# A transformer layer with product-key experts: the up side of a second token tile is gathered

## The chip, the cores and the metric

One core of a Trainium2 chip runs the whole layer in one launch. The metric is the device time of that launch in microseconds (us); three runs of the kernel before gave 1610.23, 1615.54 and 1618.56 us.

## The reference, cut to what matters

512 tokens of width 1024 pass an attention half (shift and scale by a condition, projections, differential and windowed attention, output projection, layer norm) and then an expert half. Only the expert half is touched:

```
q      = h @ w_pq                      # 8 heads, two half queries of 128 each
scores = q . sub_keys                  # 128 keys for each half
top 16 of each half -> 256 sums -> top 16 of them: idx (of 16384 experts), g = softmax
a   = gelu(u_tab[idx] . h)             # the up side: 8 x 16 = 128 experts a token
out = sum (g * a) * v_tab[idx]         # the down side
x   = LayerNorm(alpha * x + gate2 * out)
```

`u_tab` and `v_tab` have 16384 rows of 1024 floats (64 MiB each). Everything is float32.

## The kernel before, in words

The 512 tokens are four tiles of 128. **Tile 0** is done by gather: for each of its 128 choices an indirect DMA on GpSimd's queue (`fetch`, L720) brings one row of `u_tab` for each token into a buffer `gb` (512 KB, 4 buffers), and VectorE multiplies it with the token rows `h2n` and sums along the row (L728); after gelu the same is done with `v_tab`, each row added to `acc0` with its weight (L738).

**Tiles 1 to 3** are dense. The 16384 experts are 128 blocks of 128. `u_block(e)` (L749) loads a 512 KB block of `u_T` into `raw` (3 buffers, `load_raw`), splits it into a rounded part `hi` (ScalarE, L80) and a rest `lo` (VectorE, L81), both float32r with 3 buffers each, and makes the up products of 384 tokens as three float32r products for each of 8 slices (`mm3`, L90 to L92, tile `st`, two PSUM buffers). Gelu writes them to `a_r` (L756), a ring of NB + 1 = 33 buffers. `v_block(n)` (L796) loads a block of `v_tab`, splits it in the same way, multiplies `a` with the block's gate weights from `gl` (L811), splits the product into `wh` (L816) and `wl` (L817), and `v_mm` adds 18 products of 512 columns to six PSUM banks (`acc`).

The gate weights reach `gl` by a one-hot build, `make_g` (L656): for 8 tokens at a time ("a unit") VectorE makes two one-hot tables `oh0` and `oh1`, ScalarE scales the one by the gate g (8 instructions, L677), TensorE multiplies them (8 plain f32 products of 128 columns, L681), and the two PSUM banks are copied to `stage`, one by ScalarE and one by VectorE (L684). Two units make a 1 MB write to `g_d` in DRAM. A tile takes 16 units. `topk` (L596) finds the 16 choices of a tile on VectorE.

The order: first the loop over e = 0 to NB + NS - 1 = 55, which has one `u_block`, a share of `topk` (`budget`), of `make_g` (GRATE units a block) and of the gather (`c2`). The first 32 results stay in the ring; those of the NS = 24 blocks after them go to DRAM as `a_d` (`keep`, L759), through the one buffer of the ring that is left. Then the loop over n = 0 to 127: for n < 72 a `u_block` and a `v_block` ("mixed"), after that `v_block` alone; the blocks in `a_d` come last and are read back as `a_b`. A share of the gather goes along with each n. `pull(gen, us)` takes steps from a generator until the costs that it yields use up the share. All loads and stores but the gathers are issued by SyncE's queue (SP), in one order; each engine works in the order of the program.

Of the kernel before, what the change touches and what calls it, by code (L numbers as in the profile page):

```python
# [11 lines left out]
F32 = mybir.dt.float32  # L12
# [25 lines left out]
GB = 8  # L38
NS = 24
GRATE = 1.25  # L40
LAST = 6


@with_exitstack
def layer(ctx: ExitStack, tc: tile.TileContext, A, out, dbg=None):
# [17 lines left out]
    x1_d = [dram.tile([P, D], F32, name=f"x1_d{t}") for t in range(NT)]  # L63
    h2_d = dram.tile([P, D], F32, name="h2_d")
    g2_d = dram.tile([1, D], F32, name="g2_d")
    a_d = [dram.tile([P, TD], F32, name=f"a_d{e}") for e in range(NS)]
    g_d = dram.tile([NTG, P, NKEY, TG], F32, name="g_d")
# [63 lines left out]

# [1 line left out]
    at_stack = ExitStack()  # L133
# [313 lines left out]

# [1 line left out]
    lt = at_stack.enter_context(tc.tile_pool(name="lt", bufs=1, reuse_waits="tile"))  # L449
# [48 lines left out]
    def post_x(t, pre, x1):  # L498
        nc.vector.tensor_mul(x1, pre, ln1g)
        nc.vector.tensor_add(x1, x1, ln1b)  # L500
        dma(x1_d[t], x1)
        if "x1" in dbg:
            dma(dbg["x1"][t * P:(t + 1) * P, :], x1)
        if t == 0:
            sc2row = row_of(lt, scale2, "rowtmp")
            h2 = pre
            nc.vector.tensor_mul(h2, x1, sc2row)
            sh2row = row_of(lt, cols(3), "rowtmp")
            nc.vector.tensor_add(h2, h2, sh2row)
            dma(h2_d, h2)  # L510
            g2row = row_of(lt, cols(5), "rowtmp")
            dma(g2_d, g2row[0:1, :])
# [20 lines left out]

# [1 line left out]
    sel = ctx.enter_context(tc.tile_pool(name="sel", bufs=1, reuse_waits="tile"))  # L535
    vals = sel.tile([P, NT, 16, K16], F32, name="vals")
# [45 lines left out]
    q_stack.close()  # L582
    pro.close()

# [1 line left out]
    psB = ctx.enter_context(tc.tile_pool(name="psB", bufs=1, space=bass.MemoryType.PSUM, reuse_waits="tile"))  # L586
    ring_stack = ExitStack()
    ring = ring_stack.enter_context(tc.tile_pool(name="ring", bufs=1, side="right", reuse_waits="tile"))
    gath = ctx.enter_context(tc.tile_pool(name="gath", bufs=1, reuse_waits="tile"))
    acts = {}  # L590
# [5 lines left out]
    def topk(t, pool):  # L596
# [31 lines left out]
        yield 1.8  # L628
        i01 = sel.tile([P, 2, H, K16], F32, name="i01", tag="i01", bufs=2)
        for s in range(2):  # L630
# [11 lines left out]
            yield 1.4  # L642
        g = sel.tile([P, H, K16], F32, name="g", tag="g", bufs=2)
        nc.vector.tensor_sub(g, tv, tv[:, :, 0:1].to_broadcast([P, H, K16]))
# [11 lines left out]
    def make_g(t, pool):  # L656
# [9 lines left out]
        for tg in range(P // TG):  # L666
            stage = pool.tile([P, NKEY, TG], F32, name="stage", tag="stage", bufs=2)
            for q in range(TG // 8):
# [9 lines left out]
                for u in range(2):  # L678
                    ps = accbank()
                    for i in range(4):  # L680
                        nc.tensor.matmul(ps[:, i * P:(i + 1) * P], oh1[:, 4 * u + i, :], go[:, 4 * u + i, :],  # L681
                                         start=True, stop=True)
                    w = q * 8 + u * 4
                    (nc.scalar.copy if u == 0 else nc.vector.tensor_copy)(  # L684
                        stage[:, :, w:w + 4].rearrange("p i t -> p t i"), ps.rearrange("p (t i) -> p t i", t=4))
# [6 lines left out]
    budget = [0.0]  # L692

    def all_topk(pool):
        for t in (1, 0, 2, 3):
            best[t] = yield from topk(t, pool)

    def all_g(pool, tk):
        for t in range(1, NT):
            while t not in best:  # L700
                budget[0] -= next(tk, 0.0)
            yield from make_g(t, pool)

    acc0 = gath.tile([P, D], F32, name="acc0")
    h2n = gath.tile([P, D], F32, name="h2n")
    dma(h2n, h2_d)

    def gather_tile(pool):
        i01, g = best[0]
        ef = gath.tile([P, P], F32, name="ef")  # L710
        nc.vector.scalar_tensor_tensor(ef, i01[:, 0].rearrange("p h k -> p (h k)"), float(NKEY),
                                       i01[:, 1].rearrange("p h k -> p (h k)"), op0=OP.mult, op1=OP.add)
        ei = gath.tile([P, P], I32, name="ei")
        nc.vector.tensor_copy(ei, ef)
        w0 = gath.tile([P, P], F32, name="w0")
        nc.vector.tensor_copy(w0, g.rearrange("p h k -> p (h k)"))
        dots = gath.tile([P, P], F32, name="dots")
        yield 0.6

        def fetch(tab, j):  # L720
            b = gath.tile([P, D], F32, name="gb", tag="gb", bufs=4)
            nc.gpsimd.indirect_dma_start(out=b, out_offset=None, in_=A[tab],  # L722
                                         in_offset=bass.IndirectOffsetOnAxis(ap=ei[:, j:j + 1], axis=0))
            return b

        for j in range(P):
            b = fetch("u_tab", j)
            paced(nc.vector.scalar_tensor_tensor(b, b, 1.0, h2n, op0=OP.mult, op1=OP.mult,  # L728
                                                 accum_out=dots[:, j:j + 1]))
            yield 1.25  # L730
        nc.scalar.activation(dots, dots, AF.Gelu)
        nc.vector.tensor_mul(w0, w0, dots)
        for j in range(P):
            b = fetch("v_tab", j)
            if j == 0:
                paced(nc.vector.tensor_scalar_mul(acc0, b, w0[:, 0:1]))
            else:
                paced(nc.vector.scalar_tensor_tensor(acc0, b, w0[:, j:j + 1], acc0, op0=OP.mult, op1=OP.add))  # L738
            yield 1.2

    def pull(gen, us):
        while us > 0:
            try:
                us -= next(gen)
            except StopIteration:
                return us
        return us

    def u_block(e):  # L749
        hi, lo = early.pop(e) if e in early else u_split(e)  # L750
        ps = psB.tile([P, TD], F32, name="st", tag="st", bufs=2)
        for k in range(KB):
            mm3(ps, hi[:, k, :], lo[:, k, :], h2h[:, k, P:], h2l[:, k, P:], k == 0, k == KB - 1)
        pace[0], pace_next[0] = pace_next[0], split.last
        a = ring.tile([P, TD], F32, name="a_r", tag="a_r", bufs=NB + 1)
        nc.scalar.activation(a, ps, AF.Gelu)  # L756
        acts[e] = a
# [8 lines left out]
    tk = all_topk(gp)  # L766
    gg = all_g(gp, tk)
    c1 = c2 = 0.0
    gt = None
    for e in range(NB + NS):  # L770
        u_block(e)
        keep(e)
        budget[0] = pull(tk, budget[0] + (1.8 if 1 not in best else 1.8))
        if 1 in best:
            c1 += GRATE
            while c1 >= 1.0:
                c1 -= 1.0
                drain(gg, 1)
        if 0 in best:
            if gt is None:  # L780
                gt = gather_tile(gp)
            c2 = pull(gt, c2 + 0.8)
    drain(gg)
    g_stack.close()

    v_stack = ExitStack()
# [9 lines left out]
    def v_block(n):  # L796
        e = order[n]
        raw = load_raw(A["v_blk"][e], [P, D])
        if n < NKEY - 4:
            hi, lo = split(raw, [P, D])  # L800
        else:
            hi, lo = (b[:, n - NKEY + 4, :] for b in tail[1:])
            nc.scalar.copy(hi, raw)  # L803
            nc.vector.tensor_sub(lo, raw, hi.bitcast(F32))
        a = acts.pop(e)
        if a is None:
            a = vp.tile([P, TD], F32, name="a_b", tag="a_b", bufs=2)
            dma(a, a_d[e - NB])
        w = vp.tile([P, TD], F32, name="w", tag="w", bufs=2)
        i = e % GB  # L810
        nc.vector.tensor_mul(w.rearrange("p (g t) -> p g t", t=TG), a.rearrange("p (g t) -> p g t", t=TG),  # L811
                             gl[:, :, i * TG:(i + 1) * TG])
        wp, nb = (vp, 4) if n < NKEY - 3 else (tail[0], 3)
        wh = wp.tile([P, TD], F32R, name="wh", tag="wh", bufs=nb)
        wl = wp.tile([P, TD], F32R, name="wl", tag="wl", bufs=nb)
        nc.scalar.copy(wh, w)  # L816
        pace[0], pace_next[0] = pace_next[0], nc.vector.tensor_sub(wl, w, wh.bitcast(F32))  # L817
        return n, hi, lo, wh, wl
# [10 lines left out]
    for n in range(NKEY):  # L829
        if order[n] % GB == 0:  # L830
            gl = g_load(order[n])
        if n + NB + NS < NKEY:
            u_block(n + NB + NS)
            c2 = pull(gt, c2 + 3.2)
        else:
            c2 = pull(gt, c2 + 1.2)
        if n == NKEY - 16:
# [8 lines left out]
            for t in range(NT):  # L846
                dma(xr[t], x1_d[t])
            pre = [h2n] + [fin.tile([P, D], F32, name=f"pre{t}") for t in range(DT)]
            hi4 = hpool.tile([P, 4, D], F32R, name="hi4", tag="hh")
# [104 lines left out]
```

## Time and profile before

| | |
|---|---|
| median of three runs | 1615.54 us |
| span of the profiled execution (first to last instruction) | 1615.1 us |
| TensorE products, busy | 1536.0 us, 95% of the span |
| VectorE, busy | 1247.1 us, 77% |
| ScalarE, busy | 760.0 us, 47% |
| GpSimd, busy | 378.1 us, 23% |
| moved by DMA | 394.98 MB, mean 245 GB/s |
| mean granted TensorE clock | 0.981 of 2.4 GHz |

Busy shares are means over stages with different limits. Products are pipelined and overlap, so one's duration (0.33 us) is longer than the distance from its start to the next one's (0.17 us); what they cost is the distance. The same holds less strongly for VectorE and ScalarE. The DMA share is the mean over the core's 16 DMA engines.

### The profile page before, as it was taken

To read this page: it belongs to the slowest core of one execution; us is meant where nothing else is said; L and a number is where in the kernel's file an instruction comes from. 1 tells how busy PE (TensorE), PEld (TensorE's weight loads), DVE (VectorE), ACT (ScalarE), POOL (GpSimd) and SP (SyncE) were. 2 spreads that over 40 slices of the span, in tenths; PEclk is the share of its full clock that TensorE was granted. 3 is DMA by queue.
4 is the path that set the end of the run, shared out by engine and by line. 5 is a ranking of instruction groups with operands and counts; after the bars stand their busy time and mean duration, and the time that the engine had idled before them with its cause. 6 is when DMAs were issued, how large, how long until landed. Compare 5 with 4: busy or idle time off the path is not lost.

```text
span 1615.1 us, 22297 instructions
## 1 busy us (share of the span) xinstructions
PE 1536.0 (95%) x7837; PEld 1340.0 (83%) x7837; DVE 1247.1 (77%) x2519; ACT 760.0 (47%) x1346; POOL 378.1 (23%) x274
## 2 busy tenths in 40 slices
PE   7999898999998989998899999999999999999997
PEld 5677776889888888998788999988988898888875
DVE  7897666999898887766777777777868776787687
ACT  2565533234897998963233333333333333333341
POOL 0000000000011010104444443444535442434200
PEclk9999999999999999999999999999999999999999
DMA  8855542223366465689989889899889996889962
GB/s 302 289 187 181 170 156 82 89 79 116 107 219 213 155 232 190 219 282 359 313 304 329 291 311 319 297 321 312 320 289 324 322 306 246 286 300 310 374 204 76
DMA packets 154497, 394.98 MB, mean 245 GB/s; under 512 B 12305, under 2 KB 69009, under 8 KB 151186
## 3 DMA queue, kind: packets, MB, share of 16 engines
q1 hardware_dynamic: 117522, 259.33, 47.2%
q0 software_dynamic: 36864, 134.23, 23.0%
q8 instruction: 61, 1.00, 0.2%
q14 instruction: 50, 0.41, 0.1%
HBM read 358.91 MB, written 34.61 MB: 244 GB/s over the span
## 4 chain that ended last, share of the span: by engine, by line
PE 62%; issue 10%; DVE 10%; ACT 9%; DMA 7%; POOL 2%; SPq 0%; DVEq 0%; POOLq 0%; ACTq 0%
PE acc L91 9%; PE acc L90 9%; PE acc L92 9%; PE st L92 6%; PE st L91 6%; PE st L90 6%; ACT go L677 5%; PE bank L90 4%; PE bank L91 4%; PE bank L92 4%; DMA raw<-u_T 2%; DMA a_b<-a_d 2%; DVE lo L81 2%; ACT stage L684 1%; POOL gb L722 1%
## 5 line engine op out<-in xcount | busy, mean ns | idle before, releaser
L80 ACT CAST hi<-raw 128x1024 fp32r<-128x1024 f32 x286 | 300.3, 1051 | 359.8 <-PE st L91 191.3
L81 DVE TENSOR_TENSOR lo<-raw,hi 128x1024 fp32r<-128x1024 f32 x286 | 348.3, 1219 | 94.8 <-ACT hi L80 94.4
L90 PE MATMUL st<-h2h,hi 128*128 128x384 f32 x1024 | 352.4, 344 | 9.7 <-ACT a_r L756 5.8
L92 PE MATMUL st<-h2h,lo 128*128 128x384 f32 x1024 | 350.9, 343 | 5.6 <-DVE lo L81 5.5
L91 PE MATMUL st<-h2l,hi 128*128 128x384 f32 x1024 | 349.5, 341 | 0.0
L722 POOL DMA_INDIRECT gb<-u_tab,ei x128 | 173.2, 1353 | 623.2 <-DVE gb L728 354.6
L91 PE MATMUL acc<-lo,wh 128*128 128x512 f32 x768 | 304.3, 396 | 3.2 <-DVE lo L81 3.0
L90 PE MATMUL acc<-hi,wh 128*128 128x512 f32 x768 | 303.5, 395 | 0.4 <-ACT hi L803 0.4
L92 PE MATMUL acc<-hi,wl 128*128 128x512 f32 x768 | 303.8, 396 | 0.0
L722 POOL DMA_INDIRECT gb<-v_tab,ei x128 | 194.9, 1523 | 269.8 <-DVE acc L738 250.5
L90 PEld LDWEIGHTS st<-h2h,hi 128*128 128x128 f32 x1024 | 196.2, 192 | 15.2 <-ACT a_r L756 7.4
L816 ACT CAST wh<-w 128x384 fp32r<-128x384 f32 x128 | 65.6, 514 | 292.0 <-PE acc L91 273.6
L92 PEld LDWEIGHTS st<-h2h,lo 128*128 128x128 f32 x1024 | 196.0, 191 | 8.3 <-DVE lo L81 8.3
L91 PEld LDWEIGHTS st<-h2l,hi 128*128 128x128 f32 x1024 | 196.0, 191 | 3.2
L91 PEld LDWEIGHTS acc<-lo,wh 128*128 128x128 f32 x768 | 144.3, 188 | 36.5 <-DVE lo L81 4.3
L92 PEld LDWEIGHTS acc<-hi,wl 128*128 128x128 f32 x768 | 144.3, 188 | 34.5
L817 DVE TENSOR_TENSOR wl<-w,wh 128x384 fp32r<-128x384 f32 x128 | 71.1, 556 | 131.5 <-ACT wh L816 131.5
L90 PEld LDWEIGHTS acc<-hi,wh 128*128 128x128 f32 x768 | 144.1, 188 | 32.4 <-ACT hi L803 0.8
L677 ACT ACTIVATE go<-oh,iT 128x128 f32<-128x128 bf16 x384 | 166.4, 530 | 5.9 <-DVE eq L637 3.2
L738 DVE SCALAR_TENSOR_TENSOR acc<-gb,w,acc 128x1024 f32<-128x1024 f32 x127 | 162.2, 1277 | 1.2 <-DMA gb<-v_tab,ei 1.1
L728 DVE SCALAR_TENSOR_TENSOR gb<-gb,h2n 128x1024 f32<-128x1024 f32 x128 | 154.1, 1217 | 7.6 <-DMA gb<-u_tab,ei 7.5
L681 PE MATMUL acc<-go,oh 128*128 128x128 f32 x768 | 123.1, 294 | 15.2 <-ACT go L677 10.2
(206 smaller groups left out, 1854.5 us busy)
## 6 DMA issues: line engine op xcount, KB each, us to landing
raw<-u_T SPq DMA_DIRECT2D x128, 512.0 KB, 5.2
raw<-v_blk SPq DMA_DIRECT2D x128, 512.0 KB, 4.5
wada<-w_adaT SPq DMA_DIRECT2D x48, 512.0 KB, 4.5
g_d<-stage SPq DMA_DIRECT2D x24, 1024.0 KB, 5.4
gl<-g_d SPq DMA_DIRECT2D x16, 1536.0 KB, 13.1
raw<-w_pqT SPq DMA_DIRECT2D x16, 512.0 KB, 3.5
raw<-w_inT SPq DMA_DIRECT2D x10, 512.0 KB, 4.3
a_d<-a_r SPq DMA_DIRECT2D x24, 192.0 KB, 4.1
```

The costliest lines, as they stand in the source:

```text
L80: nc.scalar.copy(hi, src)
L81: split.last = nc.vector.tensor_sub(lo, src, hi.bitcast(F32))
L90: nc.tensor.matmul(ps, lh, rh, start=first, stop=False)
L91: nc.tensor.matmul(ps, lh, rl, start=False, stop=False)
L92: nc.tensor.matmul(ps, ll, rh, start=False, stop=last)
L677: nc.scalar.activation(go[:, i, :], oh0[:, :, i], AF.Copy, scale=iT[:, 2, t0 + i:t0 + i + 1])
L681: nc.tensor.matmul(ps[:, i * P:(i + 1) * P], oh1[:, 4 * u + i, :], go[:, 4 * u + i, :], start=True, stop=True)
L722: nc.gpsimd.indirect_dma_start(out=b, out_offset=None, in_=A[tab], in_offset=bass.IndirectOffsetOnAxis(ap=ei[:, j:j + 1], axis=0))
L728: paced(nc.vector.scalar_tensor_tensor(b, b, 1.0, h2n, op0=OP.mult, op1=OP.mult, accum_out=dots[:, j:j + 1]))
L738: paced(nc.vector.scalar_tensor_tensor(acc0, b, w0[:, j:j + 1], acc0, op0=OP.mult, op1=OP.add))
L816: nc.scalar.copy(wh, w)
L817: pace[0], pace_next[0] = pace_next[0], nc.vector.tensor_sub(wl, w, wh.bitcast(F32))
```

## The change

Tile 1 now takes its up side by gather, like tile 0, and its down side stays dense. Its gathered activation is multiplied into its gate weights before `make_g(1)`, so that `gl` holds for tile 1 the finished weight, and `v_block` uses that without a dense activation. The dense up products have 256 columns (TU) in place of 384, and for 75 of the 128 blocks they are 8 plain f32 products on the unsplit `raw` with a joined copy `h2f` of the tokens, in place of a split and 24 float32r products. NS goes from 24 to 72, so the first loop has 104 blocks and the mixed part 24; GRATE, the shares of the gather and of `topk`, and the order of the tiles are set anew; `gb` has 6 buffers; both copies of a unit are ScalarE's. The diff, cut:

```diff
-NS = 24
-GRATE = 1.25
+NS = 72
+GRATE = 0.62
+TU = 2 * P
+GBUF = 6
-        if t == 0:                                   # post_x: token rows for the gather
+        if t < 2:
             sc2row = row_of(lt, scale2, "rowtmp")
...
+    h2f = gath.tile([P, KB, TU], F32, name="h2f")
+    nc.vector.tensor_add(h2f, h2h[:, :, TU:].bitcast(F32), h2l[:, :, TU:].bitcast(F32))
...
-                    (nc.scalar.copy if u == 0 else nc.vector.tensor_copy)(
+                    nc.scalar.copy(
                         stage[:, :, w:w + 4].rearrange("p i t -> p t i"), ps.rearrange("p (t i) -> p t i", t=4))
...
     def all_topk(pool):
-        for t in (1, 0, 2, 3):
+        for t in (1, 2, 3, 0):
             best[t] = yield from topk(t, pool)
+            if t < 2:
...                                                   # indices ei and weights w of tile t
+                rows[t] = ei, w
     def all_g(pool, tk):
-        for t in range(1, NT):
+        for t in (2, 3):
...
             yield from make_g(t, pool)
+        while not weighted:
+            yield None
+        best[1] = best[1][0], rows[1][1].rearrange("p (h k) -> p h k", k=K16)
+        yield from make_g(1, pool)
...
+    def gather_tiles():
+        yield from gather_up(1)                       # 128 rows of u_tab, gelu, w *= dots
+        weighted.append(True)
+        yield from gather_up(0)
+        ei, w = rows[0]
         for j in range(P):
-            b = fetch("v_tab", j)
+            b = fetch("v_tab", ei, j)
...
     def u_block(e):
+        ps = psB.tile([P, TU], F32, name="st", tag="st", bufs=2)
+        if e % 2 and e not in early or e >= NB + NS:
+            raw = load_raw(A["u_T"][e], [P, KB, P])
+            for k in range(KB):
+                nc.tensor.matmul(ps, raw[:, k, :], h2f[:, k, :], start=k == 0, stop=k == KB - 1)
+        else:
+            hi, lo = early.pop(e) if e in early else u_split(e)
+            for k in range(KB):
+                mm3(ps, hi[:, k, :], lo[:, k, :], h2h[:, k, TU:], h2l[:, k, TU:], k == 0, k == KB - 1)
+            pace[0], pace_next[0] = pace_next[0], split.last
...
     for e in range(NB + NS):
         u_block(e)
         keep(e)
-        budget[0] = pull(tk, budget[0] + (1.8 if 1 not in best else 1.8))
-        if 1 in best:
+        budget[0] = pull(tk, budget[0] + (3.0 if 1 not in best else 1.4))
+        if 2 in best:
             c1 += GRATE
...
-            c2 = pull(gt, c2 + 0.8)
+        if 1 in rows:
+            c2 = pull(gt, c2 + 2.2)
+    pull(tk, 1e9)
+    while not weighted:
+        next(gt)
     drain(gg)
...
-        nc.vector.tensor_mul(w.rearrange(...), a.rearrange(...), gl[:, :, i * TG:(i + 1) * TG])
+        gi = gl[:, :, i * TG:(i + 1) * TG]
+        nc.vector.tensor_mul(w.rearrange(...), a.rearrange(...), gi[:, P // TG:])
-        nc.scalar.copy(wh, w)
-        pace[0], pace_next[0] = pace_next[0], nc.vector.tensor_sub(wl, w, wh.bitcast(F32))
+        nc.scalar.copy(wh[:, 0:P].rearrange("p (g t) -> p g t", t=TG), gi[:, 0:P // TG])
+        nc.scalar.copy(wh[:, P:], w)
+        nc.vector.tensor_sub(wl[:, 0:P].rearrange(...), gi[:, 0:P // TG], wh[:, 0:P]...)
+        pace[0], pace_next[0] = pace_next[0], nc.vector.tensor_sub(wl[:, P:], w, wh[:, P:].bitcast(F32))
...
-            c2 = pull(gt, c2 + 3.2)                   # mixed
+            c2 = pull(gt, c2 + 3.4)
         else:
-            c2 = pull(gt, c2 + 1.2)                   # v_block alone
+            c2 = pull(gt, c2 + 2.2)
```

`pull` also returns at once when a generator yields None. The two yields of `gather_up` and of the down side cost 1.25 each (before 1.25 and 1.2).

## Rows read from the trace of the kernel before

**Rows 1.** Windows: length, PE, PEld, DVE, ACT, POOL busy (count), PEclk, DMA share, GB/s.
```profile
460.00:690.00 230.00, 212.25 (x1309) 196.64 (x1308) 186.07 (x304) 210.73 (x407) 25.20 (x23) 0.99 0.60 208
850.00:1300.00 450.00, 448.59 (x2245) 403.97 (x2244) 341.18 (x421) 155.53 (x217) 206.35 (x141) 1.00 0.89 314
...
1600.00:1650.00 50.00, 4.79 (x21) 3.55 (x19) 10.79 (x18) 0.00 (x0) 0.54 (x1) 0.91 0.06 21
```
**Rows 2.** Windows, gelu (L756) alone: length, ACT busy (count), PEclk, DMA share, GB/s.
```profile
460.00:690.00 230.00, 16.94 (x31) 0.99 0.60 208
...
362.00:740.00 378.00, 32.22 (x57) 0.97 0.57 197
```
**Rows 3.** Timeline: start us, duration us, engine, line, operation, tiles, form; TensorE's products.
```profile
355.17 1.06 PE L556 MATMUL bank<-skT,qT 128*128 128x128 f32 x8
355.98 0.48 PE L90 MATMUL bank<-h2h,hi 128*128 128x512 f32 x1
...
864.12 0.33 PE L91 MATMUL st<-h2l,hi 128*128 128x384 f32 x1
...
864.29 0.33 PE L92 MATMUL st<-h2h,lo 128*128 128x384 f32 x1
...
866.96 0.40 PE L91 MATMUL acc<-lo,wh 128*128 128x512 f32 x1
...
867.19 0.40 PE L92 MATMUL acc<-hi,wl 128*128 128x512 f32 x1
```
**Rows 4.** Timeline: VectorE, two row products of the gather back to back.
```profile
865.12 1.22 DVE L728 SCALAR_TENSOR_TENSOR gb<-gb,h2n 128x1024 f32<-128x1024 f32 x1
...
866.26 1.22 DVE L728 SCALAR_TENSOR_TENSOR gb<-gb,h2n 128x1024 f32<-128x1024 f32 x1
```
**Rows 5.** Timeline: ScalarE, parts of two build units, a split and a gelu.
```profile
666.13 1.09 ACT L684 COPY stage<-acc 128x512 f32<-128x512 f32 x1
666.97 5.60 ACT L677 ACTIVATE go<-oh,iT 128x128 f32<-128x128 bf16 x13
672.42 1.10 ACT L80 CAST hi<-raw 128x1024 fp32r<-128x1024 f32 x1
673.36 0.54 ACT L756 ACTIVATE a_r<-st 128x384 f32<-128x384 f32 x1
```
**Rows 6.** Groups by line and form: count, busy us, mean ns, idle before.
```profile
L671 DVE TENSOR_TENSOR oh<-iTb,iota 128x1024 bf16<-128x1024 bf16 x48 | 32.9, 688 | 33.3 <-ACT go L677 33.3
...
L817 DVE TENSOR_TENSOR wl<-w,wh 128x384 fp32r<-128x384 f32 x128 | 71.1, 556 | 131.5 <-ACT wh L816 131.5
```
**Rows 7.** Windows, tiles cand and eq of `topk` alone: length, DVE busy (count), the rest.
```profile
362.00:790.00 428.00, 36.23 (x268) 0.97 0.62 215
...
362.00:790.00 428.00, 32.64 (x48) 0.97 0.62 215
```
**Rows 8.** Timelines of ScalarE and of SP's issues (SPq): gelu and the store a_d.
```profile
718.45 0.49 ACT L756 ACTIVATE a_r<-st 128x384 f32<-128x384 f32 x1 [2.30 <-DMA a_d<-a_r]
...
723.17 0.49 ACT L756 ACTIVATE a_r<-st 128x384 f32<-128x384 f32 x1 [3.30 <-DMA a_d<-a_r]
...
718.96 0.32 SPq L761 DMA_DIRECT2D a_d<-a_r  x1
...
723.69 3.27 SPq L761 DMA_DIRECT2D a_d<-a_r  x1
```
**Rows 9.** Windows: the two stretches in which DMA was fullest (columns of Rows 1).
```profile
1490.00:1520.00 30.00, 30.00 (x130) 24.15 (x129) 21.77 (x26) 9.92 (x14) 10.06 (x6) 1.00 1.03 404
730.00:790.00 60.00, 55.38 (x276) 51.14 (x277) 47.62 (x72) 20.06 (x30) 28.92 (x21) 0.94 1.01 352
```
**Rows 10.** DMA issues by tile: count, KB each, median us from issue to landing.
```profile
raw<-v_blk SPq DMA_DIRECT2D x128, 512.0 KB, 4.5
...
gl<-g_d SPq DMA_DIRECT2D x16, 1536.0 KB, 13.1
...
a_d<-a_r SPq DMA_DIRECT2D x24, 192.0 KB, 4.1
```

More of the change, by code (lines that the diff above doesn't have):

```diff
@@ L63, in layer @@
     x1_d = [dram.tile([P, D], F32, name=f"x1_d{t}") for t in range(NT)]
-    h2_d = dram.tile([P, D], F32, name="h2_d")
+    h2_d = [dram.tile([P, D], F32, name=f"h2_d{t}") for t in range(2)]
     g2_d = dram.tile([1, D], F32, name="g2_d")
-    a_d = [dram.tile([P, TD], F32, name=f"a_d{e}") for e in range(NS)]
+    a_d = [dram.tile([P, TU], F32, name=f"a_d{e}") for e in range(NS)]
     g_d = dram.tile([NTG, P, NKEY, TG], F32, name="g_d")
@@ L509, in post_x @@
             nc.vector.tensor_add(h2, h2, sh2row)
-            dma(h2_d, h2)
+            dma(h2_d[t], h2)
+        if t == 0:
             g2row = row_of(lt, cols(5), "rowtmp")
@@ L532, in layer @@
     at_stack.close()
-    sel = ctx.enter_context(tc.tile_pool(name="sel", bufs=1, reuse_waits="tile"))
+    gath = ctx.enter_context(tc.tile_pool(name="gath", bufs=1, reuse_waits="tile"))
+    sel_stack = ExitStack()
+    sel = sel_stack.enter_context(tc.tile_pool(name="sel", bufs=1, reuse_waits="tile"))
     vals = sel.tile([P, NT, 16, K16], F32, name="vals")
@@ L588, in layer @@
     ring = ring_stack.enter_context(tc.tile_pool(name="ring", bufs=1, side="right", reuse_waits="tile"))
-    gath = ctx.enter_context(tc.tile_pool(name="gath", bufs=1, reuse_waits="tile"))
     acts = {}
@@ L628, in topk @@
         yield 1.8
-        i01 = sel.tile([P, 2, H, K16], F32, name="i01", tag="i01", bufs=2)
+        i01 = sel.tile([P, 2, H, K16], F32, name=f"i01_{t}")
         for s in range(2):
@@ L642, in topk @@
             yield 1.4
-        g = sel.tile([P, H, K16], F32, name="g", tag="g", bufs=2)
+        g = sel.tile([P, H, K16], F32, name=f"g{t}")
         nc.vector.tensor_sub(g, tv, tv[:, :, 0:1].to_broadcast([P, H, K16]))
@@ L692, in layer @@
     budget = [0.0]
+    rows = {}
     def all_topk(pool):
-        for t in (1, 0, 2, 3):
+        for t in (1, 2, 3, 0):
             best[t] = yield from topk(t, pool)
+            if t < 2:
+                i01, g = best[t]
+                ef = gath.tile([P, P], F32, name="ef", tag="ef", bufs=1)
+                nc.vector.scalar_tensor_tensor(ef, i01[:, 0].rearrange("p h k -> p (h k)"), float(NKEY),
+                                               i01[:, 1].rearrange("p h k -> p (h k)"), op0=OP.mult, op1=OP.add)
+                ei = gath.tile([P, P], I32, name=f"ei{t}")
+                nc.vector.tensor_copy(ei, ef)
+                w = gath.tile([P, P], F32, name=f"w{t}")
+                nc.vector.tensor_copy(w, g.rearrange("p h k -> p (h k)"))
+                rows[t] = ei, w
+                yield 0.6
+    weighted = []
+    spare = []
     def all_g(pool, tk):
-        for t in range(1, NT):
+        for t in (2, 3):
             while t not in best:
@@ L702, in all_g, with fetch, gather_up @@
             yield from make_g(t, pool)
+        while not weighted:
+            yield None
+        best[1] = best[1][0], rows[1][1].rearrange("p (h k) -> p h k", k=K16)
+        yield from make_g(1, pool)
     acc0 = gath.tile([P, D], F32, name="acc0")
[L705 to L724, printed above, removed]
+    def fetch(tab, ei, j):
+        b = gath.tile([P, D], F32, name="gb", tag="gb", bufs=GBUF)
+        nc.gpsimd.indirect_dma_start(out=b, out_offset=None, in_=A[tab],
+                                     in_offset=bass.IndirectOffsetOnAxis(ap=ei[:, j:j + 1], axis=0))
+        return b
+    def gather_up(t):
+        while t not in rows:
+            yield None
+        ei, w = rows[t]
+        h2n = gath.tile([P, D], F32, name="h2n", tag="h2n", bufs=1)
+        dma(h2n, h2_d[t])
+        spare.append(h2n)
+        dots = gath.tile([P, P], F32, name="dots", tag="dots", bufs=1)
         for j in range(P):
-            b = fetch("u_tab", j)
+            b = fetch("u_tab", ei, j)
             paced(nc.vector.scalar_tensor_tensor(b, b, 1.0, h2n, op0=OP.mult, op1=OP.mult,
@@ L731, in gather_tile @@
         nc.scalar.activation(dots, dots, AF.Gelu)
-        nc.vector.tensor_mul(w0, w0, dots)
+        nc.vector.tensor_mul(w, w, dots)
+    def gather_tiles():
[3 more added lines that the diff above has]
+        ei, w = rows[0]
         for j in range(P):
-            b = fetch("v_tab", j)
+            b = fetch("v_tab", ei, j)
             if j == 0:
-                paced(nc.vector.tensor_scalar_mul(acc0, b, w0[:, 0:1]))
+                paced(nc.vector.tensor_scalar_mul(acc0, b, w[:, 0:1]))
             else:
-                paced(nc.vector.scalar_tensor_tensor(acc0, b, w0[:, j:j + 1], acc0, op0=OP.mult, op1=OP.add))
-            yield 1.2
+                paced(nc.vector.scalar_tensor_tensor(acc0, b, w[:, j:j + 1], acc0, op0=OP.mult, op1=OP.add))
+            yield 1.25
     def pull(gen, us):
@@ L743, in pull @@
             try:
-                us -= next(gen)
+                cost = next(gen)
             except StopIteration:
                 return us
+            if cost is None:
+                return 0.0
+            us -= cost
         return us
     def u_block(e):
[L750 to L755, printed above, removed]
+        ps = psB.tile([P, TU], F32, name="st", tag="st", bufs=2)
[8 more added lines that the diff above has]
+            pace[0], pace_next[0] = pace_next[0], split.last
+        a = ring.tile([P, TU], F32, name="a_r", tag="a_r", bufs=NB + 1)
         nc.scalar.activation(a, ps, AF.Gelu)
@@ L767, in layer @@
     gg = all_g(gp, tk)
+    gt = gather_tiles()
     c1 = c2 = 0.0
-    gt = None
     for e in range(NB + NS):
@@ L778, in layer @@
                 drain(gg, 1)
-        if 0 in best:
-            if gt is None:
-                gt = gather_tile(gp)
-            c2 = pull(gt, c2 + 0.8)
+        if 1 in rows:
[3 more added lines that the diff above has]
+        next(gt)
     drain(gg)
     g_stack.close()
+    sel_stack.close()
     v_stack = ExitStack()
@@ L806, in v_block @@
         if a is None:
-            a = vp.tile([P, TD], F32, name="a_b", tag="a_b", bufs=2)
+            a = vp.tile([P, TU], F32, name="a_b", tag="a_b", bufs=2)
             dma(a, a_d[e - NB])
-        w = vp.tile([P, TD], F32, name="w", tag="w", bufs=2)
+        w = vp.tile([P, TU], F32, name="w", tag="w", bufs=2)
         i = e % GB
-        nc.vector.tensor_mul(w.rearrange("p (g t) -> p g t", t=TG), a.rearrange("p (g t) -> p g t", t=TG),
-                             gl[:, :, i * TG:(i + 1) * TG])
+        gi = gl[:, :, i * TG:(i + 1) * TG]
+        nc.vector.tensor_mul(w.rearrange("p (g t) -> p g t", t=TG), a.rearrange("p (g t) -> p g t", t=TG), gi[:, P // TG:])
         wp, nb = (vp, 4) if n < NKEY - 3 else (tail[0], 3)
@@ L815, in v_block @@
         wl = wp.tile([P, TD], F32R, name="wl", tag="wl", bufs=nb)
-        nc.scalar.copy(wh, w)
-        pace[0], pace_next[0] = pace_next[0], nc.vector.tensor_sub(wl, w, wh.bitcast(F32))
+        nc.scalar.copy(wh[:, 0:P].rearrange("p (g t) -> p g t", t=TG), gi[:, 0:P // TG])
+        nc.scalar.copy(wh[:, P:], w)
+        nc.vector.tensor_sub(wl[:, 0:P].rearrange("p (g t) -> p g t", t=TG), gi[:, 0:P // TG],
+                             wh[:, 0:P].bitcast(F32).rearrange("p (g t) -> p g t", t=TG))
+        pace[0], pace_next[0] = pace_next[0], nc.vector.tensor_sub(wl[:, P:], w, wh[:, P:].bitcast(F32))
         return n, hi, lo, wh, wl
@@ L847, in layer @@
                 dma(xr[t], x1_d[t])
-            pre = [h2n] + [fin.tile([P, D], F32, name=f"pre{t}") for t in range(DT)]
+            pre = [spare[-1]] + [fin.tile([P, D], F32, name=f"pre{t}") for t in range(DT)]
             hi4 = hpool.tile([P, 4, D], F32R, name="hi4", tag="hh")
```

## The prediction, made before the changed kernel was run

> **What bounds the kernel now.** I read the page's shares and its 40 slices first, then the busy time by stretch, then groups, timelines and DMA. The expert half is 1250 of the 1615 us. It starts with the first up product at 364 us (the timeline of TensorE), and has two regimes. In the first loop, at 460 to 690 us, ScalarE is busy 210.7 of 230 us and TensorE 212.3 [rows 1], and the 31 gelus [rows 2] make it 7.4 us a block: ScalarE's build units (1.25 a block) set it. By 740 us 57 blocks are through [rows 2]. In the mixed loop TensorE is busy 448.6 of 450 us, VectorE 76%, DMA 0.89 full at 314 GB/s [rows 1]: TensorE alone sets it, 24 products at 0.17 us and 18 at 0.23 us apart [rows 3], 8.2 us a block. `v_block` alone is 18 x 0.23 = 4.14 us. TensorE is done by 1605 us [rows 1]; 10 us of layer norm follow. So TensorE's saving is real only in the second loop, and there DMA has one tenth left.
>
> **The change, part by part.** All in the profiled execution, whose 1615.1 us is the median of the runs shown (1615.54).
>
> *Start.* Two more row builds (16 f32 products of 128 columns at 0.2 us [rows 3], 3 us) and the addition that makes `h2f`, 2048 columns on VectorE at 1.14 us for 1024 [rows 4], 2.3 us: 5 us (0 if hidden behind the split work of that stage, 10 if waits come with them). First up product at 364 + 5 = 369 us.
>
> *An up block.* Split: 24 products, by columns 0.17 x 256/384 = 0.115 us, 2.8 us (bounds: 4.1 if the distance doesn't shrink; 2.7). Plain f32: four of 128 columns take 355.98 - 355.17 = 0.81 us [rows 3], 0.2 us each; 256 columns are not in the trace: bounds 0.2 (nothing for the columns) and 0.46; I take 0.43, near the proportional end, as the float32r rows follow columns (0.17 and 0.23 for 384 and 512). 8 x 0.43 = 3.4 us. Blocks alternate, so 3.1 us in place of 4.1. A plain block spares 0.94 us of ScalarE [rows 5] and 1.14 of VectorE, but holds its `raw` until TensorE has read it.
>
> *Loop one, 104 blocks in place of 56.* From block 7 on each block carries 2.2/1.25 = 1.76 gathered rows, from about block 18 0.62 build units. Prices: a row product 1.14 us of VectorE, two in sequence [rows 4]; a unit on VectorE 1.14 + 0.69 [rows 4, 6]; on ScalarE 8 x 0.42 + two copies at 0.84 = 5.0 us [rows 5], where before it had one copy. `topk` costs VectorE 36.2 + 32.6 us for two tiles' names [rows 7], with the small rest about 85 for four, 21 a tile against 17.1 in its own accounting.
> - Blocks 0 to 6: `topk` at 3.0 x 21/17.1 = 3.7 us and a split, 4.5 us on VectorE, 32 us.
> - Blocks 7 to 31: VectorE 0.57 + 2.0 + 1.4 x 1.23 = 4.3 us, from block 18 on 5.4 with 0.62 units; with small losses 4.4 and 5.6: 11 x 4.4 + 14 x 5.6 = 127 us (110 to 145).
> - Blocks 32 to 103: here the added wait counts. 32 ring buffers are full, so gelu of block e + 1 waits until the store of block e has landed. The trace has that loop bare: gelu at 718.45, store issued 718.96, next gelu 723.17, waiting on that store [rows 8]: 4.7 us. NS = 72 has 71 such steps, not 23. Behind the waiting gelu on ScalarE stand the casts and the build unit; behind the store on SP the next `raw` loads. A block without a unit takes the 4.7 us; one with a unit takes ScalarE 5.0 + 0.5 (half a split) + 0.3 (gelu) = 5.8 us, which hides the store. The ring lets no slack pass from one to the other: 0.62 x 5.8 + 0.38 x 4.7 = 5.4 us. VectorE (0.57 + 2.0 + 1.1 = 3.7) and TensorE (3.1 + 1.0) have room. DMA: 0.524 MB `raw`, 0.131 store, 0.325 for `g_d`, 1.76 x 0.524 gathered = 1.90 MB, 4.7 us at 404 GB/s, 5.4 at 352 [rows 9]. So three limits lie within a microsecond; I take 5.6 us, 403 us in all. Bounds: 4.9 (353 us); 6.6 (475 us), when SP's issue itself takes 3.27 us, as at 723.69 [rows 8].
>
> Loop one: 32 + 127 + 403 = 562 us, so it ends at 931. Before, 57 blocks had taken 376.
>
> *Crossover.* `make_g(1)` can't start before the 128 rows of tile 1 are done (128/1.76 = 73 blocks, about block 80), and its 16 units last to block 104. The first `gl` holds all tiles, so it waits for the last `g_d`; it takes 13.1 us to land [rows 10], behind which TensorE has one or two up blocks. Before, the builds were done several blocks early. 12 us (0 to 20).
>
> *Mixed, 24 in place of 72.* TensorE 3.4 + 4.14 = 7.5 us. `raw` has 3 buffers: the load of V(n+1) needs the buffer that up block n is read from. So over two blocks: 7.5 us, the landing, 3.2 us for split and queue: (7.5 + L + 3.2)/2. With L = 4.5 us [rows 10] that is 7.6; with 6.5 it is 8.6, and DMA is fuller here (2.67 MB a block). I take 8.2: 197 us (181 to 228).
>
> *V alone.* Of 384 gathered rows 171 went in loop one, 24 x 3.4/1.25 = 65 in the mixed part; 148 are left, 84 blocks at 1.76. VectorE: 1.14 for `lo`, 2.0 for rows, and `w` and two `wl` of 256 and 128 columns, 0.40 + 0.40 + 0.27 by the 0.556 for 384 [rows 6], 4.2 us. TensorE 4.14. DMA: 0.524 + 0.197 (`gl`) + 0.923 = 1.64 MB, for the 52 blocks with `a_b` 1.77 MB. At 404 GB/s that is 4.1 and 4.4 us, at 352 4.7 and 5.0 [rows 9]. Three engines at one height; I take 4.5 and 4.8: 32 x 4.5 + 52 x 4.8 = 394 us (bounds 363 and 411). Then 20 blocks at 4.14, 83 us, and 10 us of tail.
>
> The Trainium skill (SBUF — State Buffer, Summary: rules for kernel authors) says to reckon HBM to SBUF transfers with about 358 GB/s, which speaks against 67 MB more of gathers. By that figure V alone would be 4.6 and 5.0 us, 11 us more. The 404 GB/s over 30 us [rows 9] contradict it as a ceiling for one core.
>
> Sum: 369 + 562 + 12 + 197 + 394 + 83 + 10 = **1627 us**, 12 us (0.7%) over before. TensorE sheds some 130 us of up products, but the expert half moves 76 MB more (128 gathers of 0.524 MB, and the stores and loads of `a_d`), and each stage is then set by something else.
>
> **Rivals.**
> - *Overlap holds* (faster): queues run deep enough that each stage goes at its busiest engine. Loop one's late blocks 4.9, mixed 7.5, V 4.2 and 4.4, no crossover, blocks 7 to 31 at 4.8: 369 + 32 + 120 + 353 + 181 + 363 + 83 + 10 = 1511 at the limit; with half of my losses kept 1560. For it: TensorE ran 450 us without a gap at 0.89 DMA, and 404 GB/s was reached. Against: 352 GB/s at a share of 1.01, where TensorE had gaps [rows 9].
> - *The store loop jams* (slower): when DMA is full, SP's issues take 3 us, the store's landing grows, ScalarE stands in front of the units, and `raw` comes late: 6.6 us for late blocks, 9.0 mixed, V at 352 GB/s: 369 + 32 + 127 + 475 + 20 + 216 + 411 + 83 + 10 = 1743; I put it at 1720. It decides from a late block over 6 us on.
> - *A ceiling under 360 GB/s* as a rule of this core: the bytes of V alone by it, 32 x 4.6 + 52 x 5.0, 1638.
> - *The products don't get shorter* (the change doesn't do what it says): 256 columns at 0.17 us like 384. 1.3 us more on 53 blocks; late blocks then need 4.8 us of TensorE, under 5.6, so nearly all of it is hidden: 1632.
>
> The store loop is for me the likeliest new bound, since it is seen bare in the trace and has no slack; against it stands only that units hide it in six blocks of ten.
>
> **How the numbers follow.** Forecast 0.44 (1590 to 1665 of its own), overlap 0.30, jam 0.18, ceiling 0.05, products 0.03. A measurement of this kernel tells about 0.5%, 8 us, from no change. Faster than 1607: 0.27 from the overlap case and 0.11 from the low side of the forecast, 0.38. Within: 0.15. Slower than 1624: 0.23 of the forecast, the jam's 0.18 and 0.06 of the last two, 0.47. The range 1550 to 1705 leaves out the low end of the overlap and the high end of the jam, about 0.1 each. The forecast's time is 1627.
>
> **What would show it.** Right: gelus 4.7 to 5 us apart in the late blocks without a unit, each released by the store; ScalarE idle ahead of gelu for some 60 us in all; loop one ending about 930; gaps of TensorE in V alone ending on `lo` or on gathered rows; DMA above 350 GB/s there. Wrong: late blocks at 5 us or less, or TensorE without gaps in V alone (overlap); plain products more than 0.46 or float32r ones more than 0.13 us apart (prices); a granted clock that falls to 1.2 GHz in loop one for long, where it was 0.99 of 2.4 GHz [rows 1], as TensorE now rests a quarter of each block.

## The result, and the profile after

The changed kernel takes 1715.0 us (four runs, 1709.7 to 1718.8) against 1615.0: 1.062 times as long, interval 1.059 to 1.065. The forecast of 1627 was too low by 88 us, and the range (to 1705) too. Of the rivals the jam, priced at 1720, came nearest.

The stretches of the changed kernel, columns as in [rows 1]: loop one from block 32 on, the mixed part, v alone before and with `a_b`, and v alone after the last gathered row.

```profile
541.00:975.00 434.00, 343.18 (x2077) 309.07 (x2076) 276.63 (x434) 271.49 (x515) 180.26 (x133) 0.93 0.89 321
987.00:1182.00 195.00, 178.61 (x770) 149.46 (x769) 127.70 (x237) 44.88 (x98) 80.39 (x67) 0.94 0.94 331
1182.00:1338.00 156.00, 139.53 (x574) 112.90 (x573) 129.41 (x190) 50.44 (x96) 83.32 (x55) 0.92 0.91 319
1338.00:1621.00 283.00, 232.76 (x940) 184.70 (x940) 211.93 (x307) 85.13 (x158) 125.55 (x77) 0.90 0.93 320
1621.00:1705.00 84.00, 83.04 (x361) 67.13 (x359) 56.40 (x96) 27.67 (x52) 1.09 (x2) 1.00 0.50 152
```

No engine is full in the second, third and fourth row: TensorE 92, 89 and 82%, VectorE 65 to 83%. In the mixed part of before TensorE had 99.7% at nearly the same DMA load [rows 1]. Only DMA stands near 0.9 throughout (0.89 to 0.94). Where the gathers stop (last row), TensorE is full again. The page's chain of the work that ended last, by engine and by line, points the same way:

```profile
DMA 32%; PE 30%; DVE 17%; ACT 12%; issue 7%; SPq 1%; POOL 0%; DVEq 0%; ACTq 0%; POOLq 0%
DMA a_d<-a_r 11%; DMA raw<-v_blk 9%; DMA a_b<-a_d 6%; ACT go L683 4%; DVE acc L764 4%; PE bank L92 4%; PE bank L93 4%; PE bank L94 4%; PE st L783 4%; DMA raw<-u_T 3%; DVE lo L83 3%; PE acc L93 3%; PE acc L94 3%; PE acc L92 3%; ACT stage L690 2%
```

On the page of before that chain was 62% TensorE and 7% DMA. Moved: 472.56 MB, before 394.98. Who waited for whom (total us, times, longest), in loop one (400 to 950 us), first the engines, then SP's queue:

```profile
ACT a_r L790 <- DMA a_d<-a_r: 85.2, 35, 6.1
ACT hi L82 <- DMA raw<-u_T: 81.2, 28, 10.0
...
PE st L783 <- ACT a_r L790: 57.0, 27, 4.8
...
SPq L795 <- ACT a_r L790: 263.1, 65, 8.3
SPq L88 <- PE st L783: 64.0, 15, 8.4
```

and from 1160 to 1610 us, in v alone (the first 22 us are still mixed). SP (last two rows) stands at loads of `raw` until VectorE has read the buffer, and at the loads of `a_b`:

```profile
ACT hi L82 <- DMA raw<-v_blk: 110.4, 27, 14.7
...
DVE w L848 <- DMA a_b<-a_d: 68.1, 15, 12.6
...
SPq L88 <- DVE lo L83: 109.9, 39, 9.8
SPq L844 <- DMA a_b<-a_d: 65.0, 14, 9.9
```

The store loop of [rows 8] is there, as forecast (L790 is gelu). Three gelus, then SP's stores (L795) between them:

```profile
695.90 0.38 ACT L790 ACTIVATE a_r<-st 128x256 f32<-128x256 f32 x1 [0.62 <-DMA a_d<-a_r]
701.32 0.39 ACT L790 ACTIVATE a_r<-st 128x256 f32<-128x256 f32 x1
707.94 0.38 ACT L790 ACTIVATE a_r<-st 128x256 f32<-128x256 f32 x1 [5.28 <-DMA a_d<-a_r]
...
696.31 0.33 SPq L795 DMA_DIRECT2D a_d<-a_r  x1
...
701.73 0.32 SPq L795 DMA_DIRECT2D a_d<-a_r  x1
```

The last gelu waited 5.28 us for the store issued at 701.73, and from gelu to gelu that block took 6.6 us. TensorE was done with the block's products by 705.5 us, so the store set it.

### The profile page after: what moved, and what is told of

It is laid out like the page before. It is cut to its first block, busy times and chain, and to the rows that moved or that the text cites. A ratio compares the mean times of both kernels' runs of the same rounds, so it can differ in the third digit from the quotient of the medians.

```text
span 1715.1 us, 21754 instructions
## 1 busy us (share of the span) xinstructions
PE 1462.7 (85%) x7269; PEld 1226.5 (72%) x7269; DVE 1257.6 (73%) x2787; ACT 737.5 (43%) x1452; POOL 553.6 (32%) x402
## 2 busy tenths in 40 slices
DMA packets 187042, 472.56 MB, mean 276 GB/s; under 512 B 15921, under 2 KB 84913, under 8 KB 183730
## 4 chain that ended last, share of the span: by engine, by line
DMA 32%; PE 30%; DVE 17%; ACT 12%; issue 7%; SPq 1%; POOL 0%; DVEq 0%; ACTq 0%; POOLq 0%
DMA a_d<-a_r 11%; DMA raw<-v_blk 9%; DMA a_b<-a_d 6%; ACT go L683 4%; DVE acc L764 4%; PE bank L92 4%; PE bank L93 4%; PE bank L94 4%; PE st L783 4%; DMA raw<-u_T 3%; DVE lo L83 3%; PE acc L93 3%; PE acc L94 3%; PE acc L92 3%; ACT stage L690 2%
## 5 line engine op out<-in xcount | busy, mean ns | idle before, releaser
L734 POOL DMA_INDIRECT gb<-u_tab,ei x256 | 338.7, 1323 | 589.2 <-DVE gb L748 354.4
L83 DVE TENSOR_TENSOR lo<-raw,hi 128x1024 fp32r<-128x1024 f32 x211 | 257.5, 1221 | 216.8 <-ACT hi L82 213.1
L783 PE MATMUL st<-h2f,raw 128*128 128x256 f32 x1200 | 302.2, 405 | 79.0 <-ACT a_r L790 60.3
L783 PEld LDWEIGHTS st<-h2f,raw 128*128 128x128 f32 x1200 | 237.8, 204 | 120.9 <-ACT a_r L790 67.1
L748 DVE SCALAR_TENSOR_TENSOR gb<-gb,h2n 128x1024 f32<-128x1024 f32 x256 | 305.4, 1220 | 5.5 <-DMA gb<-u_tab,ei 3.6
L92 PE MATMUL st<-h2h,hi 128*128 128x256 f32 x424 | 133.3, 314 | 35.1 <-ACT a_r L790 34.2
L94 PE MATMUL st<-h2h,lo 128*128 128x256 f32 x424 | 130.3, 307 | 12.2 <-DVE lo L83 12.2
L93 PE MATMUL st<-h2l,hi 128*128 128x256 f32 x424 | 126.8, 299 | 0.0
L92 PEld LDWEIGHTS st<-h2h,hi 128*128 128x128 f32 x424 | 88.3, 208 | 43.3 <-ACT a_r L790 41.1
L687 PEld LDWEIGHTS acc<-go,oh 128*128 128x128 f32 x768 | 98.8, 195 | 16.1 <-ACT go L683 8.7
```

The costliest lines, as they stand in the source:

```text
L83: split.last = nc.vector.tensor_sub(lo, src, hi.bitcast(F32))
L92: nc.tensor.matmul(ps, lh, rh, start=first, stop=False)
L93: nc.tensor.matmul(ps, lh, rl, start=False, stop=False)
L94: nc.tensor.matmul(ps, ll, rh, start=False, stop=last)
L783: nc.tensor.matmul(ps, raw[:, k, :], h2f[:, k, :], start=k == 0, stop=k == KB - 1)
```

## The experiments

All times are medians; every run has the kernel before beside it on the same chip (1613 to 1614 us), and ratios are to that. The changed kernel is at 1.062; gains are counted from its 1715.0 us. Profile lines are from one execution of each run.

**Nine free ring buffers (`free9`).**

```diff
-NB = 32
+NB = 24
...
-NS = 72
+NS = 80
...
-        a = ring.tile([P, TU], F32, name="a_r", tag="a_r", bufs=NB + 1)
+        a = ring.tile([P, TU], F32, name="a_r", tag="a_r", bufs=NB + 9)
```

> The ring keeps its 33 buffers, but 24 results stay in it (before 32) and 80 go to DRAM (before 72), so that 9 buffers are free for the stores and not one. Theory S (the single free ring buffer: gelu waits for the store of the block before, SP's loads stand behind the store): ScalarE's wait of gelu for a_d, 85 us in 400 to 950, goes under 10, the late blocks of loop one come down from 6.0 to about 5.4 us, the whole to 1670 to 1685. Theory D (the bytes: DMA 0.9 full and more): 8 stores and 8 loads more, so 1710 to 1725, the wait only moves to raw. Theory G (bursts of the gl load stop SP's queue in the second loop): no change in loop one from it, 1705 to 1720.

1679.5 us, ratio 1.040 (1.035 to 1.045): 35 us less, as S expects. Blocks 32 to 103 take 394 us in place of 434, and ScalarE no longer waits for `a_d`; it waits for `raw` instead. The first two rows are its longest waits in loop one, the third the window of those blocks:

```profile
ACT hi L82 <- DMA raw<-u_T: 132.1, 36, 10.7
ACT a_r L790 <- PE st L94: 30.2, 9, 10.5
...
546.00:940.00 394.00, 339.86 (x2085) 307.36 (x2084) 276.90 (x432) 269.07 (x515) 182.27 (x133) 0.94 0.94 354
```

DMA has risen from 321 to 354 GB/s, and the wait has moved to it. S was the nearer limit, D stands right behind: what D expected of the wait came true, its time did not.

**The gl load in pieces (`gl_pieces`).**

```diff
-            gl = g_load(order[n])
+            gl = gl_next if n else g_load(order[n])
...
+                gl_next = vp.tile([P, NTG, GB * TG], F32, name="gl", tag="gl", bufs=2)   # for the next eight blocks
...
+            dma(gl_next[:, g0:g0 + NTG // GB, :],        # an eighth of it with each block
...
```

> The gl load of 1536 KB, one in eight blocks, is cut into eight of 192 KB (three token groups each), one a block, for the next eight blocks; same bytes and same 512-byte runs. Theory G: the gaps of 9 to 18 us between v blocks at each eighth block vanish, v alone with gathers goes from 5.2 to about 4.5 us a block, the whole to 1640 to 1665. Theory D: the same bytes at the same rate, the gaps are spread over the blocks, 1705 to 1715. Theory S: nothing in loop one, 1715.

1707.7 us, ratio 1.058 (1.054 to 1.062): 7 us, little more than the noise, as the intervals of this ratio and of 1.062 (1.059 to 1.065) overlap. The load does stop SP's queue: in the changed kernel, in v alone, the issue that follows the gl load takes 13 us, and the next ones come at once behind it:

```profile
1328.53 0.60 SPq L829 DMA_DIRECT2D gl<-g_d  x1
1332.89 13.17 SPq L88 DMA_DIRECT2D raw<-v_blk  x1
1346.10 0.91 SPq L844 DMA_DIRECT2D a_b<-a_d  x2
```

But G falls as a cause of its own: with the burst spread, v alone with `a_b` goes from 283 to 276 us, and from 320 to 328 GB/s only.

**Without tile 1's u rows (`no_u1_rows`), without tile 0's v rows (`no_v0_rows`), without both (`no_rows_u1_v0`).**

```diff
+        if t == 1:
+            fixed = fetch("u_tab", ei, 0)     # tile 1: one gather, in place of 128
...
-            b = fetch("u_tab", ei, j)
+            b = fetch("u_tab", ei, j) if t == 0 else gath.tile([P, D], F32, name="gb", tag="gb", bufs=GBUF)
...
+        b = fetch("v_tab", ei, 0)             # tile 0: the same
         for j in range(P):
-            b = fetch("v_tab", ei, j)
```

> Leaves out 127 of the 128 gathers from u_tab for tile 1 (67 MB less); VectorE's 128 row products stay, on one fixed row, so tile 1's weights are not the reference's. Theory D: loop one loses its DMA limit, blocks 32 to 80 come down from 6.0 to 5.2 us or less and the whole by 40 to 60 us, to 1655 to 1675. Theory S: the single buffer still makes gelu wait, shorter, as the store lands in about 3.5 us and not 5.1; at most 25 us less, 1690 or more. Theory G: loop one is not its place, 1715.

> Leaves out 127 of the 128 gathers from v_tab for tile 0 (67 MB less, nearly all in v alone); VectorE's sums stay, on one fixed row. Theory D: v alone falls to TensorE's 4.14 us a block without gaps, 65 to 80 us less, 1635 to 1650. Theory G: the gaps at each gl load stay in part, as SP's queue is still stopped by its 3072 runs: 20 to 40 us less, 1675 to 1695. Theory S: no change.

> Leaves out both sets of gathers, 127 rows of u_tab for tile 1 and 127 of v_tab for tile 0 (133 MB less than the changed kernel, 57 less than the kernel before); VectorE's work stays. Theory D: the two gains (54 and 92 us) add, as they lie in different loops: 1560 to 1575, under the kernel before, so TensorE's saving shows once the bytes are gone. Theory S for loop one: its share of the store loop stays, 1565 at best. If the new structure itself (104 blocks ahead of the second loop, split engines) were what costs, it would stay over 1600.

1661.3, 1622.6 and 1570.9 us; ratios 1.029 (1.025 to 1.033), 1.005 (1.003 to 1.007) and 0.972 (0.970 to 0.975). The gains are 54 and 92 us, and together 144: they add. VectorE and TensorE carried out as many instructions in all of them as in the changed kernel. Windows, first of `no_u1_rows` in loop one, then of `no_v0_rows` in v alone:

```profile
530.00:920.00 390.00, 328.35 (x2070) 298.90 (x2069) 275.77 (x427) 270.13 (x514) 83.56 (x59) 0.96 0.73 255
```

```profile
1182.00:1338.00 156.00, 156.00 (x690) 129.18 (x689) 152.07 (x222) 61.91 (x117) 4.57 (x3) 1.00 0.68 216
```

The second is to be read against the third row of the first fence, over the same 156 us: TensorE 156.0 and not 139.5, 690 products and not 574, though VectorE is at 97%. So VectorE, which I had at 4.2 us a block, keeps TensorE's 4.1, and the gathered rows are what v alone waits for. With both sets gone, at 339 MB, the change beats the kernel before by 43 us: TensorE's saving is real.

The number of bytes alone doesn't explain the loss. `no_u1_rows` moves 405.94 MB, only 11 more than the kernel before, and is still 47 us slower. It matters beside what the rows lie: of the 127 sums of tile 0's v rows after the first, the kernel before has 83 beside its mixed blocks of 8.2 us and 44 in v alone. The changed kernel has all 127 in v alone, beside blocks of 4.1 us, as its 24 mixed blocks, in place of 72, are still taken up by tile 0's u rows. No run set the shares of the gather otherwise, so whether a better order gets some of this back is not shown.

In loop one the rows and the single buffer limit together: blocks 32 to 103 fall from 434 us to 394 with the buffers (`free9`) and to 390 without the rows, though there gelu still waits 59.9 us for `a_d` from 400 to 950 us (`no_rows_u1_v0`: 63.9). No run removed both.

**All up blocks split (`all_split`).**

```diff
-        if e % 2 and e not in early or e >= NB + NS:    # plain f32 on raw
+        if False:
```

> Undoes the plain f32 products: all 128 up blocks are split and use 24 float32r products of 256 columns. Theory D (bytes) and S (store loop): they don't see the form of the products; ScalarE gets 0.5 and VectorE 0.6 us a block more in loop one, TensorE 0.3 us less: 1705 to 1725. Rival R (the plain products hold raw until TensorE has read it, so SP's loads come late: SP waited 94 us on plain products): SP's wait on them goes, loop one and the mixed part gain 20 us or more, 1680 to 1695.

1722.3 us, ratio 1.067 (1.063 to 1.071), so the plain products cost nothing that can be seen here, and a gain of some 7 us isn't clear of the noise, as the intervals of the two ratios overlap. R falls: SP's waits on plain products are gone, and others took their place.

**One copy of a unit on VectorE again (`copies_shared`).**

```diff
-                    nc.scalar.copy(
+                    (nc.scalar.copy if u == 0 else nc.vector.tensor_copy)(
```

> Undoes one part: one of the two copies of a build unit is VectorE's again. Theory S: late blocks with a unit take 5.0 in place of 5.8 us of ScalarE, so 0.62 x 0.8 x 72 = 35 us less at most, and 10 to 20 as the store loop's 4.7 to 5.5 us and DMA are close: 1695 to 1705. Theory D: ScalarE isn't the limit in loop one, 1710 to 1718.

1718.7 us, ratio 1.066 (1.063 to 1.068): no gain. In its profile blocks 32 to 103 take 428 us in place of 434, and block 32's gelu comes 7 us later, as VectorE has more to do. ScalarE's units, 5.8 us in my sum, are hardly what late blocks wait for.

**Four buffers for a_b (`a_b_4`).**

```diff
-            a = vp.tile([P, TU], F32, name="a_b", tag="a_b", bufs=2)
+            a = vp.tile([P, TU], F32, name="a_b", tag="a_b", bufs=4)
```

> a_b has 4 buffers in place of 2, nothing else. VectorE waited 70 us for a_b in v alone. Theory D: the wait moves to raw or to the gathered rows, as the bytes stay, 1705 to 1718. Rival L (latency: two buffers are too few for a landing of 5 to 9 us, and SP stands at the a_b load with raw behind it): v alone from block 56 on comes down from 5.4 to 4.8 us, 1685 to 1695.

1704.3 us, ratio 1.055 (1.054 to 1.057): 11 us. VectorE's wait for `a_b` is gone, and its wait for `hi`, which waits for `raw`, rises from 42 to 101 us:

```profile
DVE lo L83 <- ACT hi L82: 100.7, 15, 11.2
```

**The three mends together (`three_mends`).** Nine free buffers, pieces of gl, four `a_b`.

> The changed kernel with 9 free ring buffers, gl in eight pieces and 4 buffers for a_b, all waits that I know of eased, bytes up 2 MB. Theory D: the gains don't add, as DMA is full: 1665 to 1685. If waits of SP's queue were the cause and not bytes (S, G and L together), the gains add and more: 1640 or less. Still slower than before by D.

1657.8 us, ratio 1.028 (1.026 to 1.029). The single gains, 35 + 7 + 11, add to 53; measured 57. So they add, against what D expected, and the time lies below its 1665 to 1685; S, G and L together had expected 1640 or less, which did not come either. The profiled execution is the fastest of the five, 1645.4 us. Loop one's blocks 32 to 103, then v alone without and with `a_b`:

```profile
540.00:933.00 393.00, 336.80 (x2084) 305.73 (x2082) 276.20 (x429) 268.96 (x515) 183.68 (x132) 0.93 0.96 354
1144.00:1304.00 160.00, 142.26 (x576) 112.59 (x576) 131.73 (x193) 53.02 (x101) 78.22 (x55) 0.94 0.97 348
1304.00:1549.00 245.00, 224.38 (x935) 179.22 (x934) 211.43 (x307) 84.11 (x156) 121.56 (x77) 0.97 0.99 352
```

In all three DMA is nearly full, 0.96 to 0.99, at 348 to 354 GB/s on the mean. This is the rate that the second of [rows 9] shows at a share of 1.01. The mixed part of this run has 0.92 and 323 GB/s. So with the queues mended DMA is the limit in most of the expert half, and the kernel is still 45 us slower than before.

**The kernel before, mended (`before_mended`, and its halves).** NB = 24, NS = 32, ring NB + 9; and in `make_g`:

```diff
-                    (nc.scalar.copy if u == 0 else nc.vector.tensor_copy)(
+                    nc.vector.tensor_copy(
```

> The kernel before, with NB = 24 and NS = 32 in its ring of 33 (9 free buffers for the stores) and both copies of a build unit on VectorE. Its loop one was ScalarE's (7.4 us a block, 1.25 copies of 0.84 us in it) and had 40 us of waits by the single free buffer. By theory S, and as DMA is at 0.6 there, loop one sheds 20 to 40 us and the second loop stays TensorE's: 1575 to 1600. By D alone it changes nothing: 1610 to 1620.

> The kernel before with 9 free ring buffers alone (NB = 24, NS = 32). ScalarE's units were its limit in loop one, the store loop only at its end: 1605 to 1612. If the store was the limit: 1600 or less.

> The kernel before with both copies of a build unit on VectorE alone. If ScalarE's units set loop one, 1595 to 1607; if VectorE takes over (222 of 230 us busy in the version with both mends), 1608 to 1616.

Both: 1606.7 us, ratio 0.996 (0.994 to 0.997). Ring alone: 1612.7, ratio 0.998 (0.997 to 1.000). Copies alone: **1602.9 us, ratio 0.992** (0.990 to 0.995), the fastest complete kernel of the study. The row of `before_dve_copies` beside the first of [rows 1]:

```profile
460.00:690.00 230.00, 209.78 (x1306) 196.79 (x1304) 222.81 (x391) 186.28 (x386) 28.99 (x23) 0.98 0.59 215
```

ScalarE goes from 211 to 186 of 230 us, and VectorE takes over at 223. I had expected more of `before_mended` (1575 to 1600), and the two mends don't add. In the kernel before gelu waits for `a_d` only 20.2 us (460 to 800 us), not the 40 that I had put there.

## Why the prediction was wrong, by its own steps

- **V alone with gathers, the step that failed.** Forecast 4.5 and 4.8 us a block, 394 us, bounds 363 and 411; measured 1182 to 1621, 439 us, 4.9 and 5.4 a block. The bounds were the bytes over 404 and 352 GB/s. Both rates are from 30 and 60 us in which DMA was full [rows 9]; I put them in as what 84 blocks cost. The kernel ran at 319 and 320 GB/s, at shares of 0.91 and 0.93. The waits above fit this: VectorE, ScalarE and SP's queue each stand in order behind a late transfer, and DMA isn't kept full. `three_mends`, which eases three of these waits, gets 348 and 352 and takes 160 + 245 = 405 us for the same blocks, inside my bounds. `no_v0_rows` shows that without the gathered rows nothing holds TensorE there. 404 GB/s is a rate of short stretches: `gl_pieces` has 396 over 30 us in v alone (1350 to 1380), but over all of v alone no changed kernel with its gathers was seen above 352. The sign that I had named, DMA above 350 GB/s there, did not come.
- **Blocks 32 to 103, mis-sized.** Forecast 403 us, measured 434, 6.0 us a block, inside the bounds 353 to 475. By the jam's own sign, a late block over 6 us, it stood on the line. The store loop is confirmed: taking it away gave 35 us (`free9`), and ScalarE had stood 85 us ahead of gelu for it, where I had said some 60. What I had wrong is what stood beside it. I took ScalarE's units for it; `copies_shared` gives nothing, and in `free9` the wait moves to `raw` with DMA at 354 GB/s.
- **Blocks 0 to 31, mis-sized.** Block 32's gelu starts at 541 us and not at 528; the 13 us more lie within the 110 to 145 that I gave for blocks 7 to 31. From the first gelu to block 32's it is 167 us, and 160 without tile 1's rows (`no_u1_rows`), so about half of it comes with the rows.
- **Crossover and mixed part, right.** 12 + 197 us forecast, measured 975 to 1182, 207 us. These 2 us less, the 45, 31 and 13 more above and 1 more at the end make up the 88.
- **Start and end, right.** First gelu 3 us later than before (5 forecast); from the last gathered block to the end 94 us (93).
- **Prices, right.** The first line below has 15 records of plain products, two to a product. Less the 0.38 us of one record, 14 distances take 3.02 us, so 0.43 us a product and 3.4 us a block; float32r products are 0.12 us apart:

```profile
689.71 3.40 PE L783 MATMUL st<-h2f,raw 128*128 128x256 f32 x15
...
696.56 0.28 PE L93 MATMUL st<-h2l,hi 128*128 128x256 f32 x1
696.68 0.28 PE L94 MATMUL st<-h2h,lo 128*128 128x256 f32 x1
```

- **The jam's case.** Its 1720 came close, in part by luck, as its mechanism was right by half: SP's issues did take long (13.17 us) and the store loop's block 6.0 us, but its late blocks of 6.6, mixed ones of 9.0 and V at 352 GB/s were not what came (6.0, 8.1 and 320).
- **The ceiling from the Trainium skill.** By the Trainium skill (SBUF — State Buffer, Summary: rules for kernel authors), 358 GB/s, v alone would take an estimated 405 us. This agrees with the 352 GB/s of `three_mends` at a share of 0.99 far better than the 404 that I held against it. As a limit it isn't borne out: `three_mends` has 374 GB/s over 160 us of v alone (1240 to 1400).

So of the 100 us over the kernel before, some 57 are waits that the three mends ease. That the rest is DMA's rate fits its shares of 0.96 to 0.99 but is argued, as no run took rows out of the mended kernel. The sum behind it: 77.6 MB more at 350 GB/s are 222 us of full DMA, and the mixed part before had a tenth of it free (0.89), loop one four tenths (0.60). Against that stand some 130 us of TensorE by the forecast, some 114 by the distances measured (128 x 24 x 0.17 = 522 before, 53 x 24 x 0.12 + 75 x 3.4 = 408 now).

## What to carry to other kernels

Before work is moved from an engine to DMA, reckon the bytes of each stage against the rate that DMA holds over a long stretch with the same mix of transfers (here 350 GB/s), not against the best 30 us of the trace, and take off a tenth for queues that wait in order (here 320). Ask also what other transfers the move pushes into a tighter stage: here it pushed tile 0's v rows from blocks of 8.2 us to blocks of 4.1. A ring with one free buffer makes each result wait for the store before it. That cost 35 us over 72 stores here and nothing clear over 24 in the kernel before, so look for it wherever many results go out through a ring.

## What the runs showed of the hardware that was not expected

After a long wait TensorE also ran slower for a while. In v alone, after 10 us without a product, the first ones are 0.43 us apart, and from 4 us on 0.23 again. The granted clock was 0.50 from 1353 to 1357 us, the 1.2 GHz level, and 1.00 from 1358 to 1362:

```profile
1352.98 0.79 PE L93 MATMUL acc<-lo,wh 128*128 128x512 f32 x1 [10.01 <-DVE lo L83]
...
1354.42 0.63 PE L93 MATMUL acc<-lo,wh 128*128 128x512 f32 x1
1354.85 0.63 PE L94 MATMUL acc<-hi,wl 128*128 128x512 f32 x1
...
1358.19 0.39 PE L92 MATMUL acc<-hi,wh 128*128 128x512 f32 x1
1358.42 0.40 PE L93 MATMUL acc<-lo,wh 128*128 128x512 f32 x1
```

The granted clock of v alone, 0.92 and 0.90, means that a sixth and a fifth of it were granted at 1.2 GHz; without the v rows it was 1.00. The most that this can have cost is (1 - 0.92) x 156 + (1 - 0.90) x 283 = 41 us, if TensorE had worked all through those times, which it didn't. How much of it lengthened the kernel, and how much only filled time in which DMA caught up, stays open: no run here kept the clock up through a wait.
